# Modulation vectors summed along the free dimension on VectorE, with the result channels on partitions

## The chip, the cores and the metric

The kernel runs on one core of one Trainium2 chip. The metric is the device time of one launch, in microseconds (us). The core's engines are TensorE (PE, with its weight loads as a row of their own, PEld), VectorE (DVE), ScalarE (ACT), GpSimd (POOL) and SyncE (SP); here SP issues all loads. Each engine works through its own queue in order and waits where a semaphore tells it to.

## The reference

Four transformer layers (Fourier mixer, differential attention, latent attention, Fourier mixer, each followed by an MLP) over 256 latent and 256 context tokens of width 1024, then a second block with a mixture of experts. Each layer is steered by six modulation vectors per stream, and these are what the change is about:

```
sh_a, sc_a, g_a, sh_m, sc_m, g_m = split(silu(c)    @ mod_w[i] + mod_b[i], 6)   # latent stream
csh_a, ... , cg_m                = split(silu(c_ctx) @ mod_w[i] + mod_b[i], 6)   # context stream
h     = rms_norm(x, norm_mix_g[i]) * (1 + sc_a) + sh_a
x     = x + g_a * mixer(h)
x     = x + g_m * (relu(modulate(x, norm_mlp_g[i], sh_m, sc_m) @ w1)**2 @ w2)
```

`mod_w[i]` is 1024 x 6144 in fp32, 24 MB a layer. Layer 3 needs no context stream, and layer 2 needs only the first two vectors of it.

## The kernel before

Activations lie with channels on partitions: `x` is eight tiles of 128 channels x 512 tokens. Large products are made from split operands: every weight unit (128 x 1024) is loaded as `raw`, ACT casts it to `whi`, DVE subtracts to get `wlo`, and three matmuls (L377 to L379) make each product. An MLP (`mlp`) runs over eight chunks of 512 hidden channels. In a chunk `up` makes four groups `gk` of 24 matmuls of 512 columns; ACT takes relu and square, and ACT and DVE split the result into `hid` (L698). Then `down` makes eight groups `dn` of 12 matmuls of 512 columns, and after each of them DVE adds into `x` in two halves (L603). So a chunk has 192 matmuls on PE, and on DVE 16 `wlo` halves, four `hid` and 16 `x` additions. A `dn` group sits in one of three PSUM banks of tag "a". The order is `up(c+1)` ahead of `down(c)`.

The modulation vectors come in three ways:
- Layer 0, vectors 0 to 4, during the first Fourier mixer: `mod_steps` multiplies on PE (L524), with silu(c) as the stationary operand and weight tiles as the moving one.
- Layer 0, vector 5, by the same `mod_steps`, as a filler of the first MLP.
- Layers 1 to 3, by `mod_sums`, as a filler of the MLPs of layers 0 to 2. A tile of weights (128 input channels x 1024 results) is multiplied by silu(c), one number per partition, and added into `macc`: the first of eight tiles on ACT (L581), the others on DVE (L586), once per stream that needs it. What is left is a sum over the 128 partitions: matmuls with the 0/1 matrix `pick` (L592), an ACT copy out of PSUM (L595), four transposes (L545) and a DVE addition of the bias (L548).

A filler is a generator: `mlp` calls `next(fill)` after each `up` group and after each quarter of `down`, so many times as the layer's numbers say (one call at each place in layer 0, two at each `up` group of its first chunk). For layer 0 this makes 64 calls. Each `mod_sums` call works on one loaded tile of 512 KB; four such tiles (`mraw`) are in flight.

The queues' final order isn't the program's: a scheduler orders the instructions of each engine by a simulated timeline, and `issue_after` holds the fillers' DVE work behind the `hid` subtraction named by `s.anchors`. The order shown below is what came out of it.

Of the kernel before, what the change touches and what calls it, by code (L numbers as in the profile page):

```python
# [12 lines left out]
F32 = mybir.dt.float32  # L13
# [3 lines left out]
ALU = mybir.AluOpType  # L17
# [3 lines left out]
P = 128  # L21
# [11 lines left out]
MOD_STEP = 1024  # L33
# [171 lines left out]
def prepare(i, stages=ALL):  # L205
# [5 lines left out]
    a["mod_w"] = i["mod_w"]  # L211
# [101 lines left out]
class Builder:  # L313
    def __init__(s, ctx, tc, a, out, stages, dump):
# [28 lines left out]
        s.scale, s.behind = None, []  # L343
        s.csilu = s.fix.tile([P, 2 * NT + 30], F32, name="csilu")
        nc.vector.memset(s.csilu, 0.0)
        nc.scalar.activation(s.csilu[:, :2 * NT].rearrange("p (k r) -> p k r", r=2), s.cond, AF.Silu)
        s.pick = s.fix.tile([P, 33], F32, name="pick")
        nc.vector.memset(s.pick, 0.0)
        nc.vector.memset(s.pick[:, 1:2], 1.0)
        s.modt, s.amod = {}, {}  # L350
# [152 lines left out]
    def mod_steps(s, l, pool, parts=((0, 1), (2, 3), (4, 5)), bufs=4):  # L503
# [4 lines left out]
        def load():  # L508
            if order:
                c, kt = order.popleft()  # L510
                raws.append(pool.tile([P, UC], F32, name=f"mw{l}_{c}{kt}", tag="mraw", bufs=bufs))
                s.mod_dma = nc.sync.dma_start(raws[-1], s.a["mod_w"][l, kt * P:(kt + 1) * P, c * UC:(c + 1) * UC])
# [42 lines left out]
    def mod_sums(s, l, pool, cs=(0, 1, 2), bufs=4):  # L555
# [3 lines left out]
        raws, order = deque(), deque((c, kt, z) for c in cs for kt in range(NT) for z in range(2))  # L559

        def load():
            if order:
                c, kt, z = order.popleft()
                raws.append(pool.tile([P, UC], F32, name=f"mw{l}_{c}{kt}{z}", tag="mraw", bufs=bufs))
                c0 = c * 2048 + z * UC
                nc.sync.dma_start(raws[-1], s.a["mod_w"][l, kt * P:(kt + 1) * P, c0:c0 + UC])
# [4 lines left out]
        for c in cs:  # L571
            streams = range(2 if l == 1 or (l == 2 and c == 0) else 1)
            acc = [pool.tile([P, 2048], F32, name=f"macc{l}_{c}{r}", tag=f"macc{r}", bufs=1) for r in streams]
            for kt in range(NT):
                for z in range(2):
                    w = raws.popleft()
                    for r in streams:
                        a, k = acc[r][:, z * UC:(z + 1) * UC], s.csilu[:, 2 * kt + r:2 * kt + r + 1]
                        if kt == 0:
                            with s.tc.issue_after(s.anchors[0]):  # L580
                                nc.scalar.activation(a, w, AF.Copy, scale=k)  # L581
                        else:
                            for h in range(0, UC, MOD_STEP):
                                v = slice(h, h + MOD_STEP)
                                with s.tc.issue_after(s.anchors[1]):
                                    nc.vector.scalar_tensor_tensor(a[:, v], w[:, v], k, a[:, v], op0=ALU.mult, op1=ALU.add)  # L586
                    load()
                    yield
            ps = s.bank(f"mod{l}_{c}", "a")
            for r in streams:  # L590
                for j in range(4):
                    nc.tensor.matmul(ps[32 * j:32 * j + 32, :], s.pick[:, 1 - r:33 - r], acc[r][:, j * TOK:(j + 1) * TOK],  # L592
                                     start=r == 0, stop=r == len(streams) - 1, skip_group_check=True)
            sb = s.fix.tile([P, TOK], F32, name=f"modsb{l}_{c}", tag="tmp", bufs=4)
            nc.scalar.copy(sb, ps)  # L595
            yield
            s.mod_rows(l, 2 * c, 2, sb)
            yield
# [185 lines left out]
    def fourier(s, l, n, fill):  # L784
        nc, j = s.nc, l // 3
        modt = s.modt[l]
        with s.tc.tile_pool(name=f"four{l}", bufs=1) as ph:
# [58 lines left out]
            nc.vector.tensor_mul(gb, modt[:, 16:24, :], fb[:, j, :].unsqueeze(2).to_broadcast([P, NT, 2]))  # L846
# [1246 lines left out]
```

## Time and profile before

| | |
|---|---|
| median of 3 runs | 2010.93 us (2009.3 to 2012.24) |
| profiled execution: time, span | 2013.72 us, 2011.8 us |
| PE busy | 1962.1 us (98%) |
| PEld busy | 1671.6 us (83%) |
| DVE busy | 1481.2 us (74%) |
| ACT busy | 1100.8 us (55%) |
| mean granted TensorE clock | 0.99 |
| loads | 338.40 MB, 169 GB/s over the span |

The span runs from the first to the last instruction; 1.9 us of the execution lie around it. The chain of work that ended last goes 93% of the span through PE, mostly through `gk` and `dn` matmuls. The MLP of layer 0 begins at about 150 us and ends at about 510 us, that of layer 1 goes from about 770 to 1130 us, that of layer 2 from about 1290 to 1460 us. The profile puts an engine's busy time beside the length of a stretch, the idle time before an instruction in square brackets with what ended it, and merges neighbours of one kind into one row (x4).

### The profile page before, as it was taken

How to read it: one execution, taken by the hardware profiler on the slowest of the kernel's cores; microseconds unless marked ns; L12 is line 12 of the kernel's file. 1: busy time of each engine (PE TensorE's matmuls, PEld its weight loads, DVE VectorE, ACT ScalarE, POOL GpSimd, SP SyncE). 2: the span in 40 equal slices, each digit the busy share in tenths (PEclk: the TensorE clock that was granted, in tenths of full speed). 3: DMA queues.
4: the chain of work that ended last, by engine and by line, in shares of the span. 5: the costliest groups of instructions: out<-in, count | busy, mean ns of one | idle time of the engine just before them, and what ended most of it. 6: DMA issues, size and time to landing. Idle time of an engine off the chain costs nothing.

```text
span 2011.8 us, 31733 instructions
## 1 busy us (share of the span) xinstructions
PE 1962.1 (98%) x11858; PEld 1671.6 (83%) x11858; DVE 1481.2 (74%) x2832; ACT 1100.8 (55%) x2182; POOL 4.8 (0%) x13
## 2 busy tenths in 40 slices
PE   7999999999999999999999989999999999999997
PEld 4577878788888888877777977899999999987886
DVE  3645867687888956976666687788767777757698
ACT  4635333433678736343433377675657666565576
POOL 0000000000000000000000000000000000000000
PEclk9999999999999999999999999999999999999999
DMA  7845555453221223777665221576526655327694
GB/s 263 311 163 183 179 168 182 143 175 101 93 74 61 76 67 114 221 243 242 225 229 168 70 74 43 193 275 225 178 83 194 198 183 179 122 65 294 201 364 165
DMA packets 98108, 341.51 MB, mean 170 GB/s; under 512 B 13075, under 2 KB 14371, under 8 KB 97955
## 3 DMA queue, kind: packets, MB, share of 16 engines
q1 hardware_dynamic: 97954, 339.49, 50.7%
q8 instruction: 93, 1.52, 0.3%
q14 instruction: 61, 0.49, 0.1%
HBM read 338.40 MB, written 1.05 MB: 169 GB/s over the span
## 4 chain that ended last, share of the span: by engine, by line
PE 93%; DVE 3%; DMA 2%; ACT 1%; issue 1%; SPq 0%; DVEq 0%; ACTq 0%
PE gk L377 11%; PE gk L378 11%; PE gk L379 11%; PE dn L377 9%; PE dn L378 9%; PE dn L379 9%; PE gu L377 2%; PE gu L378 2%; PE gu L379 2%; PE mod L524 2%; PE pj L379 1%; PE pj L377 1%; PE pj L378 1%; DMA mw<-mod_w 1%; PE y L377 1%; PE y L378 1%
## 5 line engine op out<-in xcount | busy, mean ns | idle before, releaser
L369 ACT CAST whi<-raw 128x512 fp32r<-128x512 f32 (+1 forms) x731 | 430.8, 638 | 405.8 <-PE dn L379 276.1
L370 DVE TENSOR_TENSOR wlo<-raw,whi 128x512 fp32r<-128x512 f32 (+1 forms) x731 | 490.5, 708 | 107.4 <-ACT whi L369 105.1
L377 PE MATMUL gk<-hhi,whi 128*128 128x512 f32 (+2 forms) x1312 | 433.2, 333 | 3.1 <-ACT hhi L369 1.0
L378 PE MATMUL gk<-hhi,wlo 128*128 128x512 f32 (+2 forms) x1312 | 431.1, 330 | 0.2 <-DVE wlo L370 0.2
L379 PE MATMUL gk<-hlo,whi 128*128 128x512 f32 (+2 forms) x1312 | 425.4, 331 | 0.4 <-DVE hlo L468 0.4
L377 PE MATMUL dn<-hid,whi 128*128 128x256 f32 (+1 forms) x1088 | 356.7, 328 | 0.4 <-DVE x L603 0.4
L378 PE MATMUL dn<-hid,wlo 128*128 128x256 f32 (+1 forms) x1088 | 355.7, 327 | 0.0
L379 PE MATMUL dn<-hid,whi 128*128 128x256 f32 (+1 forms) x1088 | 355.1, 327 | 0.0
L377 PEld LDWEIGHTS gk<-hhi,whi 128*128 128x128 f32 x1312 | 247.8, 189 | 37.9 <-issue 4.6
L378 PEld LDWEIGHTS gk<-hhi,wlo 128*128 128x128 f32 x1312 | 248.5, 189 | 29.4 <-issue 5.0
L603 DVE SCALAR_TENSOR_TENSOR x<-dn,modt,x 128x256 f32<-128x256 f32 x384 | 174.0, 478 | 133.5 <-PE dn L379 133.3
L379 PEld LDWEIGHTS gk<-hlo,whi 128*128 128x128 f32 x1312 | 245.3, 189 | 30.8 <-issue 4.2
L586 DVE SCALAR_TENSOR_TENSOR macc<-mw,csilu,macc 128x1024 f32<-128x1024 f32 x182 | 226.4, 1276 | 1.7 <-DMA mw<-mod_w 1.7
L377 PEld LDWEIGHTS dn<-hid,whi 128*128 128x128 f32 x1088 | 204.4, 188 | 23.4 <-ACT whi L369 1.7
L378 PEld LDWEIGHTS dn<-hid,wlo 128*128 128x128 f32 x1088 | 204.8, 188 | 21.7 <-issue 1.7
L379 PEld LDWEIGHTS dn<-hid,whi 128*128 128x128 f32 x1088 | 204.0, 188 | 20.4
L695 ACT ACTIVATE relu<-gk 128x512 f32<-128x512 f32 x64 | 38.1, 595 | 108.8 <-PE gk L379 108.7
L698 DVE TENSOR_TENSOR hid<-relu,hid 128x512 fp32r<-128x512 f32 (+1 forms) x128 | 71.0, 554 | 31.4 <-ACT hid L698 29.6
L698 ACT CAST hid<-relu 128x512 fp32r<-128x512 f32 (+1 forms) x128 | 65.6, 513 | 41.9 <-PE dn L378 38.9
L697 ACT ACTIVATE relu<-relu 128x512 f32<-128x512 f32 (+1 forms) x128 | 67.2, 525 | 1.9
L392 ACT ACTIVATE sq<-x 128x256 f32<-128x256 f32 x104 | 41.5, 414 | 33.0 <-DVE x L603 25.9
L377 PE MATMUL pj<-hhi,whi 128*128 128x512 f32 (+1 forms) x144 | 54.0, 379 | 2.2 <-ACT hhi L467 2.2
(620 smaller groups left out, 3173.8 us busy)
## 6 DMA issues: line engine op xcount, KB each, us to landing
raw<-ws SPq DMA_DIRECT2D x378, 512.0 KB, 4.3
mw<-mod_w SPq DMA_DIRECT2D x192, 512.0 KB, 4.5
x<-ws SPq DMA_DIRECT2D x36, 512.0 KB, 5.4
more<-ws SPq DMA_DIRECT2D x24, 512.0 KB, 5.3
xt<-x SPq DMA_DIRECT2D x4, 512.0 KB, 4.8
raw<-ws SPq DMA_DIRECT2D x8, 256.0 KB, 2.5
out<-ht SPq DMA_DIRECT2D x4, 256.0 KB, 2.1
raw_dft_ch<-dft_ch SPq DMA_DIRECT2D x2, 384.0 KB, 4.1
```

Of the source, the lines that this page charges most:

```text
L369: s.nc.scalar.copy(hi, src)
L370: return s.nc.vector.tensor_sub(lo, src, hi.bitcast(F32))
L377: s.nc.tensor.matmul(out, lh, rh, start=f, stop=False)
L378: s.nc.tensor.matmul(out, ll, rh, start=False, stop=False)
L379: last = s.nc.tensor.matmul(out, lh, rl, start=False, stop=l)
L392: s.nc.scalar.activation(new, src, AF.Square)
L524: nc.tensor.matmul(ps[32 * j:32 * j + 32, :n], s.csilu[:, 2 * kt:2 * kt + 32], ws[j * m // 4][:, j * n % UC:j * n % UC + n], start=kt == 0 ...
L586: nc.vector.scalar_tensor_tensor(a[:, v], w[:, v], k, a[:, v], op0=ALU.mult, op1=ALU.add)
L603: s.nc.vector.scalar_tensor_tensor(s.x[:, ct, c], ps[:, c], gates[:, ct, q:q + 1], s.x[:, ct, c], op0=ALU.mult, op1=ALU.add)
L695: nc.scalar.activation(r[:, :n], ps[:, :n], AF.Relu)
L697: nc.scalar.activation(q[:, :n], r[:, :n], AF.Square)
L698: s.anchors = nc.scalar.copy(hid[c][0][:, m], q[:, :n]).ins, nc.vector.tensor_sub(hid[c][1][:, m], q[:, :n], hid[c][0][:, m].bitcast(F32)).ins
```

## The change

All of `mod_w` is handed over a second time, transposed, as `mod_wT` (result channels as rows). `mod_sums` now loads 128 result channels x 1024 input channels. `crow` holds silu(c) of each stream as a row of 1024 numbers, the same on all partitions; 16 small matmuls make it at the start, and ACT copies it out of PSUM in four pieces. One DVE instruction (L590 of the changed kernel) multiplies a tile with `crow` and adds along the free dimension; the sums land in their place in `modt`. `macc`, `pick`, the matmuls with it, the PSUM copy and the transposes are gone for layers 1 to 3, and so is ACT's part. Each of the six vectors is eight tiles; then the bias is added for the streams that were made. Vector 5 of layer 0 is made this way too. The last MLP that has a filler (layer 2) takes vectors 4 and 5 of layer 3, the one of layer 1 all of layer 2 and vectors 0 to 3 of layer 3. A mixer of layer 3 uses only the latent column of its gates. The count of loaded tiles stays at 192.

```diff
-    a["mod_w"] = i["mod_w"]
+    a["mod_w"] = i["mod_w"][stages[0] % 4]
+    a["mod_wT"] = i["mod_w"].transpose(0, 2, 1)
...
+    def cond_rows(s):
+        nc = s.nc
+        s.crow = s.fix.tile([P, 2, D], F32, name="crow")
+        for q in range(4):
+            ps = s.bank(f"crow{q}", "a")
+            for k in range(4):
+                c = 2 * (q % 2 * 4 + k) + q // 2
+                nc.tensor.matmul(ps[:, k * P:(k + 1) * P], s.csilu[:, c:c + 1].to_broadcast([P, P]), s.ident,
+                                 start=True, stop=True)
+            nc.scalar.copy(s.crow[:, q // 2, q % 2 * TOK:(q % 2 + 1) * TOK], ps)
...
+    def mod_sums(s, l, pool, vectors=range(6), bufs=4):
...
-        for c in cs:
-            streams = range(2 if l == 1 or (l == 2 and c == 0) else 1)
...
-                            with s.tc.issue_after(s.anchors[0]):
-                                nc.scalar.activation(a, w, AF.Copy, scale=k)
...
-                                    nc.vector.scalar_tensor_tensor(a[:, v], w[:, v], k, a[:, v], op0=ALU.mult, op1=ALU.add)
...
+        for c in vectors:
+            streams = range(2 if l < 2 or (l == 2 and c < 2) else 1)
+            n = len(streams)
+            for j in range(NT):
+                w = raws.popleft()
+                for r in streams:
+                    t = pool.tile([P, D], F32, name="msum", tag="msum", bufs=1)
+                    with s.tc.issue_after(s.anchors[1]):
+                        nc.vector.scalar_tensor_tensor(t, w, 1.0, s.crow[:, r], op0=ALU.mult, op1=ALU.mult,
+                                                       accum_out=s.modt[l][:, 8 * c + j, r:r + 1])
+                load()
+                if j < NT - 1:
                     yield
-            ps = s.bank(f"mod{l}_{c}", "a")
-            for r in streams:
-                for j in range(4):
-                    nc.tensor.matmul(ps[32 * j:32 * j + 32, :], s.pick[:, 1 - r:33 - r], acc[r][:, j * TOK:(j + 1) * TOK],
...
-            nc.scalar.copy(sb, ps)
-            yield
-            s.mod_rows(l, 2 * c, 2, sb)
+            m = s.modt[l][:, 8 * c:8 * c + 8, 0:n]
+            with s.tc.issue_after(s.anchors[1]):
+                nc.vector.tensor_add(m, m, s.mod_b[:, l, 8 * c:8 * c + 8].unsqueeze(2).to_broadcast([P, NT, n]))
...
-                    filler = lambda ph, f=filler: chain(s.mod_steps(0, ph, ((5,),)), f(ph))
+                    filler = lambda ph, f=filler: chain(s.mod_sums(0, ph, (5,)), f(ph))
...
-                    filler = lambda ph: chain(s.mod_sums(2, ph), s.mod_sums(3, ph, (0, 1)))
+                    filler = lambda ph: chain(s.mod_sums(2, ph), s.mod_sums(3, ph, range(4)))
...
-                    filler = lambda ph: s.mod_sums(3, ph, (2,))
+                    filler = lambda ph: s.mod_sums(3, ph, (4, 5))
```

Two places in DVE's queue and one in ACT's show what moves. First DVE before the first `x` addition of the first MLP, as it was:

```order
L698 TENSOR_TENSOR hid_1_1619<-relu_1647,hid_1_1618 128x512
L370 TENSOR_TENSOR wlo_1697<-raw_1544,whi_1696 128x512 x2
L548 TENSOR_TENSOR modt_117<-modtp_5_1692,c_mod_b 128x16
L698 TENSOR_TENSOR hid_1_1619<-relu_1688,hid_1_1618 128x512
L370 TENSOR_TENSOR wlo_1752<-raw_1569,whi_1751 128x512 x2
L698 TENSOR_TENSOR hid_1_1619<-relu_1731,hid_1_1618 128x512
L370 TENSOR_TENSOR wlo_1795<-raw_1616,whi_1794 128x512 x2
L603 SCALAR_TENSOR_TENSOR x<-dn_00_1802,modt_117,x 128x256 x2
```

The same place in the changed kernel (`msum` is the product tile that nobody reads, `modt_139` the vectors of layer 0):

```order
L702 TENSOR_TENSOR hid_1_1641<-relu_1769,hid_1_1640 128x512
L590 SCALAR_TENSOR_TENSOR msum,modt_139<-mw_55_1528,crow 128x1024 x2
L369 TENSOR_TENSOR wlo_1825<-raw_1638,whi_1824 128x512 x2
L590 SCALAR_TENSOR_TENSOR msum,modt_139<-mw_56_1551,crow 128x1024
L702 TENSOR_TENSOR hid_1_1641<-relu_1814,hid_1_1640 128x512
L590 SCALAR_TENSOR_TENSOR msum,modt_139<-mw_56_1551,crow 128x1024
L590 SCALAR_TENSOR_TENSOR msum,modt_139<-mw_57_1557,crow 128x1024
L369 TENSOR_TENSOR wlo_1863<-raw_1695,whi_1862 128x512 x2
L590 SCALAR_TENSOR_TENSOR msum,modt_139<-mw_57_1557,crow 128x1024
L597 TENSOR_TENSOR modt_139<-modt_139,c_mod_b 128x16
L590 SCALAR_TENSOR_TENSOR msum,modt_1673<-mw_00_1675,crow 128x1024
L607 SCALAR_TENSOR_TENSOR x<-dn_00_1832,modt_139,x 128x256 x2
```

From the first `hid` subtraction to the first `x` addition there are now 17 sums, 12 `wlo` halves and eight `hid` subtractions; before there were ten `wlo` halves, seven `hid` subtractions and no sum.

Next, DVE in the second `down` of that MLP, before:

```order
L603 SCALAR_TENSOR_TENSOR x<-dn_10_2186,modt_117,x 128x256 x2
L586 SCALAR_TENSOR_TENSOR macc_01_1746<-mw_060_2091,csilu,macc_01_1746 128x1024
L603 SCALAR_TENSOR_TENSOR x<-dn_11_2201,modt_117,x 128x256 x2
L586 SCALAR_TENSOR_TENSOR macc_00_1745<-mw_061_2134,csilu,macc_00_1745 128x1024
L370 TENSOR_TENSOR wlo_2217<-raw_2056,whi_2216 128x512 x2
L586 SCALAR_TENSOR_TENSOR macc_01_1746<-mw_061_2134,csilu,macc_01_1746 128x1024
L603 SCALAR_TENSOR_TENSOR x<-dn_20_2228,modt_117,x 128x256 x2
L370 TENSOR_TENSOR wlo_2259<-raw_2099,whi_2258 128x512 x2
L603 SCALAR_TENSOR_TENSOR x<-dn_21_2243,modt_117,x 128x256 x2
```

And now:

```order
L607 SCALAR_TENSOR_TENSOR x<-dn_10_2235,modt_139,x 128x256 x2
L590 SCALAR_TENSOR_TENSOR msum,modt_1673<-mw_11_1918,crow 128x1024
L607 SCALAR_TENSOR_TENSOR x<-dn_11_2250,modt_139,x 128x256 x2
L590 SCALAR_TENSOR_TENSOR msum,modt_1673<-mw_12_1962,crow 128x1024
L369 TENSOR_TENSOR wlo_2266<-raw_2099,whi_2265 128x512 x2
L590 SCALAR_TENSOR_TENSOR msum,modt_1673<-mw_12_1962,crow 128x1024
L607 SCALAR_TENSOR_TENSOR x<-dn_20_2279,modt_139,x 128x256 x2
L590 SCALAR_TENSOR_TENSOR msum,modt_1673<-mw_13_2006,crow 128x1024
L607 SCALAR_TENSOR_TENSOR x<-dn_21_2294,modt_139,x 128x256 x2
```

The pattern is the same; the sums are spread over all of the chunk, where before they stood closer together and paused at the first tiles and at the evacuations.

Last, ACT at the start of the program, where the rows `xt` of the input are squared and normalised, before:

```order
L880 ACTIVATE sq,ss<-xt 128x512
L880 ACTIVATE sq,rs_137<-xt 128x512
L880 ACTIVATE sq,ss<-xt 128x512
L880 ACTIVATE sq,rs_137<-xt 128x512
L444 ACTIVATE rsq<-ss,eps 128x2
L369 CAST hhi<-xn 128x512
L369 CAST dft_half_95<-raw_dft_half 128x516
```

And now:

```order
L884 ACTIVATE sq,ss<-xt 128x512
L884 ACTIVATE sq,rs_159<-xt 128x512
L564 COPY crow<-crow_83 128x512
L884 ACTIVATE sq,ss<-xt 128x512
L884 ACTIVATE sq,rs_159<-xt 128x512
L564 COPY crow<-crow_89 128x512
L443 ACTIVATE rsq<-ss,eps 128x2
L564 COPY crow<-crow_95 128x512
L368 CAST dft_half_117<-raw_dft_half 128x516
```

Two `crow` copies stand ahead of the first root, a third ahead of the first table's cast.

## Rows read from the trace of the kernel before

**Rows 1.** Window: length; PE, PEld, DVE, ACT, POOL busy; clock, DMA, GB/s.
```profile
176.00:300.00 124.00, 124.00 (x538) 97.79 (x538) 89.77 (x132) 49.51 (x82) 0.00 (x0) 1.00 0.56 174
```

**Rows 2.** Groups of instructions: busy us, mean ns | idle before them.
```profile
L586 DVE SCALAR_TENSOR_TENSOR macc<-mw,csilu,macc 128x1024 f32<-128x1024 f32 x182 | 226.4, 1276 | 1.7 <-DMA mw<-mod_w 1.7
...
L592 PE MATMUL mod<-macc,pick 128*32 128x512 f32 x104 | 19.3, 602 | 0.0
...
L545 PE MATMUL modtp<-ident,modsb 128*128 128x128 f32 x48 | 7.4, 273 | 0.3 <-ACT modsb L530 0.3
L595 ACT COPY modsb<-mod 128x512 f32<-128x512 f32 x9 | 5.2, 582 | 19.1 <-PE mod L592 19.1
```

**Rows 3.** Timeline of PE around one vector pair's pick matmuls: start, length, instruction.
```profile
268.39 0.39 PE L379 MATMUL gk<-hlo,whi 128*128 128x512 f32 x1
268.71 1.05 PE L592 MATMUL mod<-macc,pick 128*32 128x512 f32 x4
269.70 0.50 PE L377 MATMUL gk<-hhi,whi 128*128 128x512 f32 x1
...
273.52 0.40 PE L378 MATMUL gk<-hhi,wlo 128*128 128x512 f32 x1
273.85 1.91 PE L592 MATMUL mod<-macc,pick 128*32 128x512 f32 x12
275.69 0.50 PE L379 MATMUL gk<-hlo,whi 128*128 128x512 f32 x1
```

**Rows 4.** Timeline of PE at the transposes that follow.
```profile
280.92 0.60 PE L545 MATMUL modtp<-ident,modsb 128*128 128x128 f32 x4
281.27 0.48 PE L377 MATMUL dn<-hid,whi 128*128 128x512 f32 x1
```

**Rows 5.** Timeline of PE at the matmuls of vector 5 of layer 0.
```profile
143.49 0.39 PE L377 MATMUL gk<-hhi,whi 128*128 128x256 f32 x1 [0.49 <-ACT hhi L467]
...
153.78 1.93 PE L524 MATMUL mod<-mw,csilu 128*32 128x256 f32 x30
155.64 0.50 PE L377 MATMUL gk<-hhi,whi 128*128 128x512 f32 x1
```

**Rows 6.** Windows of the start, columns as in the first group.
```profile
0.00:20.00 20.00, 11.04 (x37) 4.81 (x38) 11.58 (x39) 14.51 (x35) 0.70 (x6) 1.00 0.83 283
...
50.00:85.00 35.00, 31.53 (x197) 21.65 (x198) 24.40 (x54) 22.93 (x58) 0.00 (x0) 1.00 0.84 310
```

**Rows 7.** Timeline of DVE at a product that is also summed along the free dimension.
```profile
1804.40 0.67 DVE L1490 SCALAR_TENSOR_TENSOR sqr<-ht 128x512 f32<-128x512 f32 x1
...
1805.00 0.08 DVE L1490 DVE_READ_ACCUMULATOR sqr<-ht 128x1 f32 x1
...
1805.18 0.16 DVE L1534 TENSOR_TENSOR ss<-ss 128x2 f32<-128x2 f32 x1
```

**Rows 8.** Timeline of DVE in the first MLP: first evacuation, then one chunk's start to the next's.
```profile
158.60 0.68 DVE L698 TENSOR_TENSOR hid<-relu,hid 128x512 fp32r<-128x512 f32 x1
...
187.70 0.88 DVE L603 SCALAR_TENSOR_TENSOR x<-dn,modt,x 128x256 f32<-128x256 f32 x2 [0.37 <-PE dn L379]
...
232.46 0.88 DVE L603 SCALAR_TENSOR_TENSOR x<-dn,modt,x 128x256 f32<-128x256 f32 x2 [0.37 <-PE dn L379]
233.25 0.68 DVE L698 TENSOR_TENSOR hid<-relu,hid 128x512 fp32r<-128x512 f32 x1
233.85 4.87 DVE L586 SCALAR_TENSOR_TENSOR macc<-mw,csilu,macc 128x1024 f32<-128x1024 f32 x4
238.63 0.87 DVE L603 SCALAR_TENSOR_TENSOR x<-dn,modt,x 128x256 f32<-128x256 f32 x2
239.42 1.27 DVE L586 SCALAR_TENSOR_TENSOR macc<-mw,csilu,macc 128x1024 f32<-128x1024 f32 x1
240.61 1.28 DVE L370 TENSOR_TENSOR wlo<-raw,whi 128x512 fp32r<-128x512 f32 x2
241.82 2.47 DVE L586 SCALAR_TENSOR_TENSOR macc<-mw,csilu,macc 128x1024 f32<-128x1024 f32 x2
```

More of the change, by code (lines that the diff above doesn't have):

```diff
@@ L32 @@
 META = 16
-MOD_STEP = 1024
 MORE = 3
@@ L343, in __init__ @@
         s.scale, s.behind = None, []
+        s.modt, s.amod = {}, {}
         s.csilu = s.fix.tile([P, 2 * NT + 30], F32, name="csilu")
@@ L346, in __init__ @@
         nc.scalar.activation(s.csilu[:, :2 * NT].rearrange("p (k r) -> p k r", r=2), s.cond, AF.Silu)
[L347 to L350, printed above, removed]
+        if stages[0] < 4:
+            s.cond_rows()
         s.acc = {}
@@ L511, in load @@
                 raws.append(pool.tile([P, UC], F32, name=f"mw{l}_{c}{kt}", tag="mraw", bufs=bufs))
-                s.mod_dma = nc.sync.dma_start(raws[-1], s.a["mod_w"][l, kt * P:(kt + 1) * P, c * UC:(c + 1) * UC])
+                s.mod_dma = nc.sync.dma_start(raws[-1], s.a["mod_w"][kt * P:(kt + 1) * P, c * UC:(c + 1) * UC])
         s.mod_tiles(l)
@@ L553, in mod_rows @@
                                                g[:, l, :].unsqueeze(2).to_broadcast([P, NT, 2]), op0=ALU.add, op1=ALU.mult)
-    def mod_sums(s, l, pool, cs=(0, 1, 2), bufs=4):
+    def cond_rows(s):
         nc = s.nc
-        raws, order = deque(), deque((c, kt, z) for c in cs for kt in range(NT) for z in range(2))
+        s.crow = s.fix.tile([P, 2, D], F32, name="crow")
[8 more added lines that the diff above has]
+        nc = s.nc
+        raws, order = deque(), deque((c, j) for c in vectors for j in range(NT))
         def load():
             if order:
[L563 to L566, printed above, removed]
+                c, j = order.popleft()
+                raws.append(pool.tile([P, D], F32, name=f"mw{l}_{c}{j}", tag="mraw", bufs=bufs))
+                r0 = c * D + j * P
+                nc.sync.dma_start(raws[-1], s.a["mod_wT"][l, r0:r0 + P])
         s.mod_tiles(l)
@@ new lines, in mod_sums @@
+        for c in vectors:
[10 more added lines that the diff above has]
+                if j < NT - 1:
+                    yield
+            m = s.modt[l][:, 8 * c:8 * c + 8, 0:n]
+            with s.tc.issue_after(s.anchors[1]):
+                nc.vector.tensor_add(m, m, s.mod_b[:, l, 8 * c:8 * c + 8].unsqueeze(2).to_broadcast([P, NT, n]))
+                if c in (1, 4):
+                    g = (s.g_mix, s.g_mlp)[c // 4]
+                    nc.vector.scalar_tensor_tensor(s.amod[l][:, c // 4, :, 0:n], m, 1.0, g[:, l, :].unsqueeze(2).to_broadcast(
+                        [P, NT, n]), op0=ALU.add, op1=ALU.mult)
@@ L845, in fourier @@
                 pass
-            nc.vector.tensor_mul(gb, modt[:, 16:24, :], fb[:, j, :].unsqueeze(2).to_broadcast([P, NT, 2]))
+            nc.vector.tensor_mul(gb[:, :, 0:1], modt[:, 16:24, 0:1], fb[:, j, :].unsqueeze(2))
             s.gemm_k8(n, s.biased(gb, modt[:, 16:24]), src=(fhi, flo), after=s.late_norm(l))
```

14 lines of the change are left out of this document (removed).

## The prediction

> **What bounds the kernel now.** I read the page's first part and the chain that ended last, then the windows, then the groups by line, and last the timelines of PE and DVE around the work that the change touches. In the first MLP PE is busy for all 124.00 us of a window, at full clock, while DVE is busy for 89.77 and ACT for 49.51 [rows 1]. One chunk there takes 44.76 us, from the first addition into x of one to that of the next (187.70 to 232.46), for 192 matmuls, so 0.233 us a matmul [rows 8]. PE is the bound of that stretch, and what is taken off its queue there shortens it, as long as DVE, which gets more to do, keeps up. ACT only loses work and isn't near its limit.
>
> **What leaves PE.** The pick matmuls stand between product matmuls without any idle time ahead of them. From the start of the product matmul before to the start of the one behind there are 1.31 us for four records and 2.17 us for twelve; less the 0.233 that the first matmul takes anyway that is 1.08 and 1.94, so 3.02 us for sixteen [rows 3]. There are 104 such records, which makes 19.6 us; their busy time, 19.3, says the same [rows 2]. The transposes hold up the next product by 0.35 us a group [rows 4], and nine groups go: 3.2 us. Of vector 5 of layer 0, thirty records in one row push the next product back by 1.86 us [rows 5]. Two records more and two transposes stand alone between products; I put them at 0.5, an estimate by the rows just used. The other 32 records of that vector lie where PE also waits for the normalised input (0.49 idle at 143.49, ended by ACT [rows 5]); at the rate of the thirty they would be worth 2.0, and I take 0.7, with 0 and 2.0 as ends. Sum: 19.6 + 3.2 + 1.9 + 0.5 + 0.7 = 25.9 us off PE's path. The evacuating ACT copies (582 ns, nine of them [rows 2]) go too, at no gain, since ACT isn't late there.
>
> **What comes at the start.** Sixteen small matmuls and four ACT copies for crow. PE is busy for only 11.04 of the first 20 us, ACT for 14.51 [rows 6], so the matmuls cost nothing and the copies may cost something: they are 512 columns wide like the copies of 582 ns [rows 2], together 2.3 us, and two stand ahead of the root that the first normalised rows wait for, a third ahead of the cast of the first table. Behind them on ACT wait the casts, and for these PE's first transform matmuls. Some of it comes back from 50 to 85 us, where PE is idle for 3.5 us and the DMA engines have their highest share, 0.84 [rows 6]: PE waits for weights there, and a delay before it shortens that wait. I take +1.0, with 0 and 2.3 as ends.
>
> **What DVE gets.** Sums were 182 and are now 16 + 96 + 64 + 48 = 224. The old one starts every 1.195 us (four from 233.85 to 238.63 [rows 8]). The new one is shown by the trace at half its width: a product of 512 columns that is also summed starts at 1804.40, the reading of its accumulator follows at 1805.00, and the next instruction, which needs the sum, starts at 1805.18, so 0.78 us in all [rows 7]. Another 512 columns cost at most half of 1.195, which gives 1.38 as the upper end; the lower is 1.195 and the 0.08 of the reading, 1.28. I take 1.32. The next sum waits for the one before, since both write the same tile msum, but that wait is in the 0.78.
>
> In a steady chunk DVE then has sixteen sums (21.1 us), eight pairs of x additions at 0.79 (238.63 to 239.42), eight pairs of wlo halves at 1.21 (240.61 to 241.82) and four hid subtractions at 0.60 (233.25 to 233.85) [rows 8]: 21.1 + 6.3 + 9.7 + 2.4 = 39.5 of 44.76 us. It fits, with 5 us to spare. That DVE may run without a pause and PE not notice is shown: from 232.46 to 241.82 DVE never waits, and four sums stand between two x additions, while the window shows PE fully busy [rows 1, 8]. The break-even is a sum of (44.76 - 18.4) / 16 = 1.65 us.
>
> [...] The product just shown has two fp32 sources in SBUF and is summed, and takes 0.60 us to its accumulator reading for 512 columns [rows 7], the old sum 1.195 for 1024 with two such sources [rows 8]; neither is at half rate, though the two sources of the first are one and the same tile. [...]
>
> One place is tight: the first up of the first MLP. Vector 5 must be ready before the first x addition, and DVE's order puts 17 sums, 12 wlo halves and 8 hid subtractions from the first hid subtraction to it: 17 x 1.32 + 12 x 0.605 + 8 x 0.60 = 34.5 us. Before, this stretch went from 158.60 to 187.70 [rows 8]. With the matmuls of vector 5 gone I let it begin at 156, so the first x addition starts at 190.5 and ends at 191.3. PE finishes the first dn about 3 us earlier than before, at 184.6, and can run two more (12 x 0.233 = 2.8 each) before it needs that bank again, at 190.2. PE stands for about 1 us, and DVE's waits for ACT in between add to it. I take +2.0, ends 0 and 5. What waits behind the sums on DVE there, besides x, is wlo of later weights; up to five units are split ahead, so this is not late first.
>
> In the second MLP the vectors with two streams come first, 32 sums in 16 calls, in 14 calls a chunk: 42.2 + 18.4 x 16/14 = 63.2 us in 51.2. Before there were 28 there and PE was as busy; the scheduler's order lets the new sums trail, and the later ones, one a call, leave room (14 x 1.32 + 18.4 = 36.9 of 44.76). I cost it at nothing; if its cover goes, up to 6 us are lost (12 behind, less two dn of slack). The loads are the same 192 tiles of 512 KB through the same four buffers, and the rows of 4 KB stay: nothing.
>
> **Sum.** -25.9 + 1.0 + 2.0 = -22.9 us. Against the profiled execution's own 2013.72 (span 2011.8 and 1.9 around it) that is 1990.8; that execution lies 2.8 above the median of the runs, 2010.93, so for the median 1988.0. The own range of this case is 1982 to 1996: the lower end has the crow copies and the stand for nothing and 2.0 for the uncertain records, and some gain from bank "a", which the pick matmuls no longer hold; the upper end has the copies at 2.3, the stand at 5 and some microseconds in the second MLP.
>
> **Rivals.** First, DVE takes most of it back. Its queue is in order, and an x addition that waits for PE makes the sums behind it late; 2.5 us lost in each of eight chunks of the first two MLPs would be 20, so 2008. For it: DVE is to go from 72% of the window to 88% of a chunk. Against it: the same pattern ran there before without a wait of PE. That the removed matmuls only filled waits of PE would end at the same place; the rows show no idle time around them [rows 3].
>
> Second, it gains more than the sum. ACT loses 26 multiplications and ten PSUM copies, and the dn groups get the third bank back whenever a pick group held it. If small waits that the busy times hide go with them, 8 to 10 us more, so 1979. Against it: PE was busy for all of the window, so few waits can be there.
>
> Third, slower: the sum runs at half rate. Two different fp32 tiles are read, and the trace shows the sum only with one tile read twice. A sum would then take 2 x 1.195 + 0.08 = 2.47 us, over the break-even of 1.65. A chunk of the first MLP would take 16 x 2.47 + 18.4 = 57.9 us instead of 44.76, over six chunks 79 us; its start 17 x 2.47 + 12.1 = 54.1 instead of 34.5, 20 us; the second MLP 96 x 2.47 + 7 x 18.4 = 366 instead of 313, 53 us. Less the 25.9 that is +126, so 2137 for the median.
>
> **Chances.** The forecast 0.74, more gain 0.07, taken back or hidden 0.12, half rate 0.07. Of the third group I count 0.05 as faster, 0.04 as within 0.2% (about what a measurement of this kernel tells from no change, 4 us) and 0.03 as slower. So faster 0.86, same 0.04, slower 0.10. The range for 8 in 10 is 1980 to 2005: it holds nearly all of the forecast, some of the gain beyond it and of what is taken back, and leaves out the half rate.
>
> **What would show it.** Right: PE's count of records lower by 104 + 64 + 38 and higher by some 32 at the start; the sums at about 1.2 us with a reading of 0.08 behind each, starting every 1.3 us; DVE near 88% of a steady chunk, PE without waits on DVE but at the first x addition of the first MLP; the second MLP shorter by about 11 us (48 of the 104 records at 3.02 for sixteen, and five of the nine groups of transposes). Wrong: sums of over 1.65 us, PE waits on x or wlo in several chunks, or a first mixer that ends some microseconds later than before.

## The result, and the profile after

The changed kernel takes 1985.45 us (median of 4 runs, 1982.98 to 1986.46), the kernel before on the same chip 2010.12 (4 runs). The ratio is 0.9866, 95% interval 0.9854 to 0.9879: 24.7 us faster, where 22.9 were forecast. The profiled execution took 1984.99 (span 1983.2). That of before (2013.72) lies 3.6 us above its median here and that of after 0.5 below its own, so the spans of the two traces differ by 28.6.

The page's first part, kernel after:

```profile
PE 1936.1 (98%) x11684; PEld 1670.4 (84%) x11684; DVE 1525.1 (77%) x3105; ACT 1070.5 (54%) x2150; POOL 4.8 (0%) x13
```

PE has 174 records fewer (11,858 before): the 104, 64 and 38 that were counted, less 32 for `crow`. The groups of DVE by line, kernel after (busy us, mean ns | idle before), answer to the old sums of [rows 2]:

```profile
L590 DVE SCALAR_TENSOR_TENSOR msum<-mw,crow 128x1024 f32<-128x1024 f32 x224 | 273.2, 1220 | 2.2 <-DMA mw<-mod_wT 1.0
...
L590 DVE DVE_READ_ACCUMULATOR msum<-mw,crow 128x1 f32 x224 | 18.7, 84 | 0.0
```

The old sum's mean was 1276 ns. Reading the accumulator is 84 ns of its own. DVE's timeline in the first MLP of after (start, length, instruction) shows what these cost in the queue, beside [rows 7, 8]:

```profile
197.01 1.22 DVE L590 SCALAR_TENSOR_TENSOR msum<-mw,crow 128x1024 f32<-128x1024 f32 x1
198.16 0.09 DVE L590 DVE_READ_ACCUMULATOR msum<-mw,crow 128x1 f32 x1
198.28 1.23 DVE L590 SCALAR_TENSOR_TENSOR msum<-mw,crow 128x1024 f32<-128x1024 f32 x1
...
202.39 1.22 DVE L590 SCALAR_TENSOR_TENSOR msum<-mw,crow 128x1024 f32<-128x1024 f32 x1
203.54 0.08 DVE L590 DVE_READ_ACCUMULATOR msum<-mw,crow 128x1 f32 x1
203.54 0.69 DVE L369 TENSOR_TENSOR wlo<-raw,whi 128x512 fp32r<-128x512 f32 x1
```

From a sum to the next sum, which writes the same tile, there are 1.27 us (197.01 to 198.28); to the start of its accumulator reading 1.15 (202.39 to 203.54). Another instruction, here a `wlo` subtraction, starts together with that reading, so beside other work a sum costs 1.15. The forecast was 1.32. Nothing is at half rate: a plain subtraction of two fp32 tiles of 1024 columns takes 1222 ns in this trace (36 of them, L369), as long as the sum.

The windows of after (length; PE, PEld, DVE, ACT, POOL busy; clock, DMA, GB/s): the stretch that answers to [rows 1], a later one, the first MLP from its first dn to its last, and the second MLP, from its normalisation (the first `st_mlp` matmul) to its last dn:

```profile
174.00:298.00 124.00, 124.00 (x533) 100.05 (x532) 116.34 (x216) 41.43 (x74) 0.00 (x0) 1.00 0.63 208
300.00:400.00 100.00, 100.00 (x430) 80.60 (x429) 86.12 (x158) 36.01 (x65) 0.00 (x0) 1.00 0.61 196
180.98:496.13 315.15, 315.15 (x1452) 258.69 (x1451) 262.21 (x492) 111.57 (x205) 0.00 (x0) 1.00 0.53 173
749.20:1115.80 366.60, 365.40 (x1756) 302.98 (x1755) 287.62 (x559) 140.33 (x264) 0.00 (x0) 1.00 0.61 201
```

The same two stretches of the MLPs in the kernel before:

```profile
184.70:509.96 325.26, 324.86 (x1512) 260.59 (x1511) 244.82 (x370) 123.71 (x218) 0.00 (x0) 1.00 0.51 160
763.50:1142.90 379.40, 378.21 (x1825) 305.20 (x1825) 275.82 (x446) 155.10 (x281) 0.00 (x0) 1.00 0.59 194
```

DVE is busy for 94% of the first stretch, and PE still for all of it: the list of PE's waits has no entry there. The first MLP is 10.1 us shorter from its first dn on (325.26 less 315.15) with DVE busy for 17 us more, the second 12.8 us (379.40 less 366.60) with DVE busy for 12 us more; its last dn in the kernel before is at 1142.9, later than the 1130 named above.

Where the 28.6 us lie shows by the same instruction in both traces, each the difference from one mark to the next: from the start to the first MLP's normalisation -2.1, on to its first dn -1.7, to the end of that MLP -10.1, second MLP -12.7, third -1.0. These are 27.6. The rest, -1.4 in the third mixer, -1.5 in the fourth and +3.1 in the fourth MLP among it, lies in code that the change leaves alone but for one DVE multiplication of gates in the fourth mixer. The steps in the mixers go with the granted clock: the fourth mixer takes 48.83 us at a mean clock of 0.93 in before, 47.32 at 0.96 in after and 45.79 at 1.00 in the last run below; the third 148.56 at 0.99 in before and 147.14 at 1.00 in after. The step in the fourth MLP doesn't, since the clock is at 1.00 there in every trace: from its normalisation to its last dn it takes 178.4 to 178.8 us in the four traces with the code of before, and 180.3 to 181.6 in all of those with the code of after but one (178.4, the run with the PE work put back). So it goes with the changed kernel; why is open. Single traces tell a stage with the change in it, but not the end to better than 3 us.

One thing was not foreseen. PE's timeline of after at the first MLP's normalisation, where vector 5 was before:

```profile
137.01 0.95 PE L418 MATMUL st_mlp<-ones,sq 128*128 128x2 f32 x8
139.26 1.19 PE L433 MATMUL r_mlp<-ident,rs_mlp 128*128 128x128 f32 x4 [1.30 <-DVE rs_mlp L451]
141.56 0.58 PE L376 MATMUL gk<-hhi,whi 128*128 128x256 f32 x1 [1.11 <-ACT hhi L466]
...
144.29 0.41 PE L377 MATMUL gk<-hhi,wlo 128*128 128x256 f32 x1
144.50 0.41 PE L376 MATMUL gk<-hhi,whi 128*128 128x256 f32 x1
...
146.26 0.28 PE L376 MATMUL gk<-hhi,whi 128*128 128x256 f32 x1
146.39 0.28 PE L377 MATMUL gk<-hhi,wlo 128*128 128x256 f32 x1
```

The windows of that stretch in after (columns as above):

```profile
138.00:140.00 2.00, 0.74 (x3) 0.77 (x4) 0.72 (x5) 0.26 (x1) 0.00 (x0) 0.81 0.96 385
140.00:142.00 2.00, 0.89 (x5) 0.59 (x4) 1.51 (x4) 1.00 (x3) 0.00 (x0) 0.50 0.90 365
142.00:144.00 2.00, 2.00 (x11) 2.00 (x11) 2.00 (x6) 1.06 (x3) 0.00 (x0) 0.50 0.03 12
144.00:146.00 2.00, 2.00 (x12) 2.00 (x11) 2.00 (x6) 1.17 (x3) 0.00 (x0) 0.50 0.00 0
146.00:148.00 2.00, 2.00 (x18) 2.00 (x18) 0.97 (x3) 0.51 (x1) 0.00 (x0) 0.99 0.00 0
```

The granted clock falls to 0.50 at about 139.2, at the end of the first wait (windows of 0.5 us have 1.00 until 139.0, 0.73 from there and 0.50 from 139.5), so the second wait isn't its reason. It is back at 146.0. Products of 256 columns start every 0.21 us meanwhile, and every 0.12 once it is back. From 141.56 to 146.00 that costs about 2 us, an estimate from these two spacings (4.44 us less 0.12/0.21 of it). In the kernel before, the same five windows have 1.00. It is no accident of one trace: all eight traces with the code of after show the lower clock between 132 and 148, and none of the four with the code of before.

### The profile page after: what moved, and what is told of

It is laid out like the page before. It is cut to its first block, busy times and chain, and to the rows that moved or that the text cites. A ratio compares the mean times of both kernels' runs of the same rounds, so it can differ in the third digit from the quotient of the medians.

```text
span 1983.2 us, 31614 instructions
## 1 busy us (share of the span) xinstructions
PE 1936.1 (98%) x11684; PEld 1670.4 (84%) x11684; DVE 1525.1 (77%) x3105; ACT 1070.5 (54%) x2150; POOL 4.8 (0%) x13
## 3 DMA queue, kind: packets, MB, share of 16 engines
HBM read 338.40 MB, written 1.05 MB: 171 GB/s over the span
## 4 chain that ended last, share of the span: by engine, by line
PE 94%; DVE 3%; ACT 2%; DMA 1%; issue 1%; SPq 0%; DVEq 0%; ACTq 0%
PE gk L376 11%; PE gk L377 11%; PE gk L378 11%; PE dn L377 9%; PE dn L376 9%; PE dn L378 9%; PE gu L376 2%; PE gu L377 2%; PE gu L378 2%; PE mod L523 2%; PE pj L376 1%; PE pj L378 1%; PE pj L377 1%; PE y L376 1%; PE y L377 1%; PE y L378 1%
## 5 line engine op out<-in xcount | busy, mean ns | idle before, releaser
L369 DVE TENSOR_TENSOR wlo<-raw,whi 128x512 fp32r<-128x512 f32 (+1 forms) x731 | 494.4, 711 | 111.0 <-ACT whi L368 109.1
L590 DVE SCALAR_TENSOR_TENSOR msum<-mw,crow 128x1024 f32<-128x1024 f32 x224 | 273.2, 1220 | 2.2 <-DMA mw<-mod_wT 1.0
L702 DVE TENSOR_TENSOR hid<-relu,hid 128x512 fp32r<-128x512 f32 (+1 forms) x128 | 71.0, 555 | 26.5 <-ACT hid L702 24.7
L391 ACT ACTIVATE sq<-x 128x256 f32<-128x256 f32 x104 | 41.6, 415 | 33.2 <-DVE x L607 25.9
```

Source lines behind the costliest of these rows:

```text
L369: return s.nc.vector.tensor_sub(lo, src, hi.bitcast(F32))
L391: s.nc.scalar.activation(new, src, AF.Square)
L590: nc.vector.scalar_tensor_tensor(t, w, 1.0, s.crow[:, r], op0=ALU.mult, op1=ALU.mult, accum_out=s.modt[l][:, 8 * c + j, r:r + 1])
L702: s.anchors = nc.scalar.copy(hid[c][0][:, m], q[:, :n]).ins, nc.vector.tensor_sub(hid[c][1][:, m], q[:, :n], hid[c][0][:, m].bitcast(F32)).ins
```

## The experiments

Theory: PE bounds both kernels in the MLPs, so the time that the removed records put between products comes off the end, and DVE's added work is hidden as long as a sum stays under 1.65 us. First rival: the records only filled slack, and the gain is ACT's or that of something freed. Second rival: DVE is already at the edge. Where a run is set against the kernel after (1985.45), the two medians come from different sessions; the kernel before moved by up to 2.3 us between these (2010.12 to 2012.41), so such a difference is no better than that.

**The pick groups and transposes twice** (kernel before). The last argument of `mod_rows` is new and says how often the transposes are issued.

```diff
-            for r in streams:
+            for r in (*streams, *streams):
                 for j in range(4):
                     nc.tensor.matmul(ps[32 * j:32 * j + 32, :], s.pick[:, 1 - r:33 - r], ...
...
-            s.mod_rows(l, 2 * c, 2, sb)
+            s.mod_rows(l, 2 * c, 2, sb, 2)
```

> The kernel before, with every pick group issued twice into the same bank and each group of transposes behind it twice; ACT and DVE do the same work as before, and the vectors come out the same. If the change gained by taking matmuls off PE's queue (my theory), the second issue costs what the first one does: 19.6 + 3.2 = 22.8 us more than before, about 2033, and PE shows the second group at about the same spacing. If the gain came mostly from ACT's lost work and from the PSUM bank and evacuation (rival), PE's extra groups cost less than 8 us.

Measured: 2028.4 us, before 2012.41, ratio 1.007 (1.0051 to 1.0088), so +16.0: between the two. PE's timeline in it, at the second half of the first pair's group:

```profile
276.46 0.40 PE L378 MATMUL gk<-hhi,wlo 128*128 128x512 f32 x1
276.79 3.63 PE L592 MATMUL mod<-macc,pick 128*32 128x512 f32 x28
280.35 0.50 PE L379 MATMUL gk<-hlo,whi 128*128 128x512 f32 x1
```

The 28 records put 3.89 us between the products (276.46 to 280.35), 3.66 over the 0.233 of one; the 12 of before put 1.94 [rows 3]. So 16 more records joined on cost 1.72, not 3.02. Summed over the trace, the spacing around picks grows by 11.2 us and that around transposes by 3.9: 15.1 against the measured 16. The three MLPs that hold them are 5.8, 7.4 and 1.4 us longer than before, 14.6 together. What stands in PE's queue does come out in the time; only the second issue was cheaper than I had said.

**The same work put back into the kernel after**, with no reader: the pick matmuls read `crow`, the transposes as well.

```diff
...
+            if l and c % 2:
+                ps = s.bank(f"mod{l}_{c}", "a")
+                for r in streams:
+                    for j in range(4):
+                        nc.tensor.matmul(ps[32 * j:32 * j + 32, :], s.pick[:, 1 - r:33 - r], s.crow[:, j % 2, ...],
+                                         start=r == 0, stop=r == n - 1, skip_group_check=True)
+                tp = s.bank(f"modtp{l}_{c}", "b")
+                for q in range(4):
+                    nc.tensor.transpose(tp[:, q * P:(q + 1) * P], s.crow[:, 0, q * P:(q + 1) * P], s.ident)
```

> The changed kernel, with the 104 pick records and 36 transposes put back on PE after every second vector of layers 1 to 3, on data that lies in SBUF and with nobody reading the result; ACT and DVE as in the changed kernel. My theory: 22.8 us come back, about 2008, that is within 4 us of the kernel before. Rival (ACT and evacuations make the gain): under 8 us come back, 1993 or less.

Measured: 1995.07, ratio 0.9907 (0.989 to 0.9923), +9.6 over the kernel after: again too little for the theory as I had priced it, too much for the rival. PE's timeline in it:

```profile
253.53 0.40 PE L381 MATMUL dn<-hid,whi 128*128 128x512 f32 x1
253.86 1.93 PE L602 MATMUL mod<-crow,pick 128*32 128x512 f32 x16
255.71 0.50 PE L379 MATMUL gk<-hhi,whi 128*128 128x512 f32 x1
```

Here `crow` is ready at any time, so all 16 records stand in one place and cost 1.95 (2.18 less 0.233); in the kernel before they stood in two, 4 and 12, for 3.02 [rows 3]. Eight in one place cost 1.08. Four such groups of sixteen and five of eight make 13.2 us, and the first twelve transposes fell into PE's wait at 143. By the trace the first MLP is 5.2 us longer from its first dn to its last, the second 7.7 and the third 1.2. The PSUM bank is held here for the matmuls alone, since no ACT copy follows; what its longer hold in the kernel before cost is not tested by itself.

**The same in the kernel before, joined**: the quarters issued in an order in which the first two can't go ahead of the others.

```diff
-                for j in range(4):
+                for j in (2, 3, 0, 1):
                     nc.tensor.matmul(ps[32 * j:32 * j + 32, :], s.pick[:, 1 - r:33 - r], ...
```

> The kernel before, with the four quarters of a pick group issued in the order 2, 3, 0, 1, so that the first two can't be issued ahead of the other two, whose sums come later. In the kernel before six of nine groups stand in two places of PE's queue; here the three with one stream stand in one, those with two streams in one or two with eight records each. Theory (what a group costs PE is a price per place in its queue, about 1.08 for up to eight records and 1.95 for sixteen, so the shortfall of the run that put the picks back on PE comes from the joined groups): 3 x 1.07 + 3 x 0.86 = 5.8 us less, so about 2006, and the spacing of the products around the picks in its trace adds up to some 14 instead of 19.6. Rival (the price is one per record and the shortfall came from elsewhere, a gap of PE that hid them): the time of the kernel before, within 1 us, and a spacing of 19 to 20.

Measured: 2009.52, before 2011.69, ratio 0.9988 (0.9973 to 1.0003): the time does not decide; 2006 would be 0.9972, just outside. PE's timeline in it:

```profile
275.30 0.39 PE L379 MATMUL gk<-hlo,whi 128*128 128x512 f32 x1
275.62 1.06 PE L592 MATMUL mod<-macc,pick 128*32 128x512 f32 x8
276.61 0.50 PE L377 MATMUL gk<-hhi,whi 128*128 128x512 f32 x1
277.04 1.07 PE L592 MATMUL mod<-macc,pick 128*32 128x512 f32 x8
278.04 0.50 PE L378 MATMUL gk<-hhi,wlo 128*128 128x512 f32 x1
```

Sixteen records as twice eight cost 1.08 and 1.20, not 3.02. All picks together put 14.8 us between the products, where the kernel before has 19.6: the price of a place is shown in the spacing. The MLPs that hold most of them are 1.7 and 2.8 us shorter, 4.5 of the 4.8 that the spacing lost, and 2.0 of that is lost in the first mixer, which the edit doesn't touch: its granted clock is 0.50 for 6.9 us there (from 53.6), which it never is there in the trace of before.

**ACT's work put back** (kernel after): 26 multiplications of 1024 columns and nine copies of 512.

```diff
+                if l and j == 0:
+                    for r in streams:
+                        idle = pool.tile([P, D], F32, name="idle", tag="idle", bufs=1)
+                        with s.tc.issue_after(s.anchors[0]):
+                            nc.scalar.activation(idle, w, AF.Copy, scale=s.csilu[:, r:r + 1])
+                if l and c % 2 and j == 7:
...
+                        nc.scalar.copy(idle[:, :TOK], s.crow[:, 0, :TOK])
```

> The changed kernel, with ACT's part put back: 26 multiplications of 128 x 1024 and nine copies of 512 columns, in about the same places, with nobody reading the result (28.2 + 5.2 us of ACT busy time). My theory: ACT isn't near its limit, so no change, 1983 to 1988. Rival: 10 us or more come back, 1995 or more.

Measured: 1982.01, ratio 0.9851 (0.9834 to 0.9867). The 26 cost ACT 1150 ns each, 30 us in all, and the time doesn't rise: what ACT lost is worth nothing that can be seen. As far as it rests on ACT, the first rival falls.

**DVE's margin**: an instruction more on DVE behind each of the 224 sums, first of 128 columns.

```diff
                                                        accum_out=s.modt[l][:, 8 * c + j, r:r + 1])
+                        nc.vector.tensor_mul(t[:, :128], w[:, :128], s.crow[:, r, :128])
```

> The changed kernel, with one more DVE multiplication of 128 columns behind every sum (224 in all), into the same product tile. That makes a sum cost about 1.27 + 0.25 = 1.5 us on DVE, under the break-even of 1.65 that the prediction worked out for a steady chunk. My theory: DVE has about 5 us to spare in a chunk of 44.76, so only the start of the first MLP pays, 17 x 0.25 = 4 us at most: 1985 to 1990. Rival (DVE is already at its limit and the queue's order makes every addition show): 224 x 0.25 = 56 us on DVE, half or more of it in the time, 2013 or more.

Measured: 1989.97, ratio 0.9886 (0.9864 to 0.9908): 4.5 over the kernel after, with intervals that overlap. In its trace both MLPs are as long as in after within 0.3 us; what is later lies in the first mixer (1.3) and the third (5.3). The last sum of the second MLP ends 57 us ahead of the third mixer, so no sum stands in it; but its mean clock is 0.97 (152.40 us) where after has 1.00 (147.14): it is at 0.50 for 10 us in all, which loses some 5. Whether the added work brought that about is not shown.

And of 512 columns:

> The changed kernel, with one more DVE multiplication of 512 columns behind every sum. A sum then costs about 1.27 + 0.70 = 1.97 us, over the break-even of 1.65. My theory: a chunk of the first MLP takes 16 x 1.97 + 18.4 = 49.9 instead of 44.76, six of them 31 us; the start of it 17 x 0.7 = 12; the second MLP 96 x 1.97 + 7 x 18.4 = 318 instead of 313, 5; together 40 to 50 us more than the changed kernel, about 2030. Rival (DVE's spare time is larger than the sum says, since a reading of the accumulator lies beside the next instruction): under 25 us more, 2010 or less.

Measured: 2020.03, ratio 1.0044 (1.0029 to 1.0058), 34.6 over the kernel after. DVE's timeline in it, first MLP:

```profile
302.69 0.68 DVE L703 TENSOR_TENSOR hid<-relu,hid 128x512 fp32r<-128x512 f32 x1
303.29 0.68 DVE L592 TENSOR_TENSOR msum<-mw,crow 128x512 f32<-128x512 f32 x1
304.01 1.23 DVE L590 SCALAR_TENSOR_TENSOR msum<-mw,crow 128x1024 f32<-128x1024 f32 x1
```

The added instruction takes the queue for 0.72 us (303.29 to 304.01), so a sum costs about 1.87, over the break-even of 1.65; with 128 columns it was some 1.4 (0.20 to 0.32 for the added one). The loss is not where I looked for it. In the chunks PE goes on without a wait, since the sums trail: the first MLP is 314.5 us long from its first dn to its last (315.2 in after), the second 366.2 (366.6). The bill comes behind the MLP. Windows in this kernel from the last dn on:

```profile
496.00:505.00 9.00, 3.43 (x17) 3.27 (x18) 9.00 (x22) 3.04 (x8) 0.00 (x0) 0.77 0.58 176
505.00:515.00 10.00, 7.66 (x49) 7.00 (x48) 10.00 (x29) 2.71 (x6) 0.00 (x0) 0.87 0.17 54
```

And in the kernel after:

```profile
496.00:505.00 9.00, 6.59 (x49) 5.80 (x48) 8.38 (x26) 5.98 (x13) 2.08 (x4) 1.00 0.50 160
```

DVE is busy throughout while PE waits (by the list of waits 4.2 us for the next normalisation, and from 550 to 561 another 10.4 for `v`, which DVE splits). From the last dn of the first MLP to the second MLP's normalisation PE is idle for 24.7 us, where after has 5.6, and busy for 8.7 us more, at a mean clock of 0.96 for 0.99: part of the bill is that lower clock, 0.77 in the first of its windows above, with PE busy for 3.43 of 9 us. At the second MLP's normalisation the kernel is 27 us behind, at the end of that MLP still 27, and at the third's normalisation 37.

**Two tiles for the products instead of one** (kernel after), so that a sum needn't wait for the one before.

```diff
-                    t = pool.tile([P, D], F32, name="msum", tag="msum", bufs=1)
+                    t = pool.tile([P, D], F32, name="msum", tag="msum", bufs=2)
```

> The changed kernel with two product tiles instead of one. In its trace a sum that follows a sum starts 1.26 to 1.27 us after it, one that follows another instruction lets that one start after 1.15: if the difference is the wait for the one product tile, sums that follow each other now start every 1.15 us. In the time this is worth nothing by my theory (DVE isn't the bound), 1983 to 1988; if DVE bounds the first MLP's start, up to 2 us less.

Measured: 1983.88, ratio 0.9861 (0.9842 to 0.9881), no change. DVE's timeline in it:

```profile
199.34 1.23 DVE L590 SCALAR_TENSOR_TENSOR msum<-mw,crow 128x1024 f32<-128x1024 f32 x1
200.49 0.09 DVE L590 DVE_READ_ACCUMULATOR msum<-mw,crow 128x1 f32 x1
200.49 1.23 DVE L590 SCALAR_TENSOR_TENSOR msum<-mw,crow 128x1024 f32<-128x1024 f32 x1
```

The next sum starts together with the reading, after 1.15 us. The shared tile costs 0.12 a sum, on an engine that has room.

**`crow` alone** (kernel before, with `cond_rows` added, called at the start, and nothing reading what it makes).

```diff
         s.modt, s.amod = {}, {}
+        s.cond_rows()
...
```

> The kernel before, with the sixteen small matmuls and four ACT copies for crow added at the start and nobody using crow. The prediction's step: +1.0 us (0 to 2.3). The changed kernel's trace rather shows the first MLP's statistics 2.1 us earlier than before: if that is due to the new order of the first matmuls and not to crow, this kernel is between 2 us faster and 1 us slower than before, and its trace shows where the first transform product and the statistics of the first MLP stand (11.09 and 120.48 us before, 11.39 and 118.41 in the changed kernel).

Measured: 2011.42, before 2012.41, ratio 0.9997 (0.9986 to 1.0009). In the trace the first MLP's normalisation starts at 118.56 against 120.48 before, 1.9 earlier rather than later. PE's waits up to 55 us, kernel before (us in total, times, longest):

```profile
PE mod L524 <- DMA mw<-mod_w: 3.1, 3, 1.6
```

The same in this run:

```profile
PE mod L525 <- DMA mw<-mod_w: 1.1, 2, 0.6
```

PE waits 2.0 us less for weights of the first vectors, which agrees in size. But that mark isn't steady: over the kernels whose code is nearly the same up to it, it lies between 120.5 and 123.5 with the code of before, and between 118.4 and 121.4 with that of after (in part of them the granted clock falls to 0.50 on the way, for 6.9 us in the two late ones of before, 122.5 and 123.5). So `crow` costs nothing that can be seen; that it brings 2 us is not shown.

**Vector 5 back on PE** (kernel after).

```diff
-                    filler = lambda ph, f=filler: chain(s.mod_sums(0, ph, (5,)), f(ph))
+                    filler = lambda ph, f=filler: chain(s.mod_steps(0, ph, ((5,),)), f(ph))
```

> The changed kernel, with vector 5 of layer 0 made by matmuls as before. The prediction counts 3.1 us for taking it off PE (1.9 + 0.5 + 0.7), and 2.0 of them given back since PE waits for DVE at the first x addition: by that this kernel is 1 us slower than the changed one, and the first MLP's DVE has 16 sums less. The changed kernel's trace shows another loss: with these matmuls gone PE idles from 137.96 to 141.56, but for one small product, and its granted clock is 0.50 from 140 to 146, where it was 1.00 before. If that costs more than the matmuls do, this kernel is as fast or up to 2 us faster, and its trace shows the clock at 1.00 there.

Measured: 1988.32, ratio 0.9882 (0.9863 to 0.9902): 2.9 slower, within the intervals. That is nearer to the 1 us slower than to the rival, which also asked for a clock of 1.00 in its trace. From the normalisation to the first dn its trace is 2.8 longer than that of after, so taking the vector off PE is worth about that, the lower clock of either trace counted in. Windows in it:

```profile
142.00:144.00 2.00, 1.70 (x10) 1.35 (x6) 2.00 (x6) 1.34 (x4) 0.00 (x0) 0.50 0.97 346
144.00:146.00 2.00, 2.00 (x16) 1.10 (x16) 2.00 (x6) 1.34 (x3) 0.00 (x0) 0.73 0.86 348
```

The clock falls here too, for a shorter time. So that vector 5's records are gone is not the whole reason for the fall; why the kernel before kept 1.00 stays open. With the same records as before but this clock the stretch is 1.2 us longer than in before (65.4 for 64.2).

**One vector more** (kernel after): vector 4 of layer 0 by sums as well, in the first mixer, with its tiles in an area that is free there.

```diff
-            fill = s.mod_steps(0, ph, ((0, 1), (2,), (3, 4)))
+            area = []
+            fill = s.mod_first(ph, area)
...
+        for _ in s.mod_steps(0, ph, ((0, 1), (2,))):
+            yield
+        a, b = s.mod_steps(0, ph, ((3,),)), s.mod_sums(0, ph, (4,), 3, area)
+        for _ in a:
+            next(b, None)
+            yield
...
```

> The kernel after, and in the first Fourier mixer vector 4 of layer 0 is also computed by sums on DVE (16 more sums, tiles in an area of SBUF that is free there); vector 3 stays on PE, alone. PE then issues 8 groups of eight 256-column records instead of 16 groups of four 512-column records. Theory (PE is the bound of this stretch, it was busy for all of 60 to 118.4 us in the kernel after, and DVE has room, 28.6 of 58.4 us busy): 16 x about 1.05 less 8 x about 0.65, so some 11 us less on PE, of which 8 to 11 show in the time: 1974 to 1978. DVE's 16 sums are 16 x 1.2 = 19 us and fit. Rival: the sums lie ahead of DVE's part of the normalisation in its queue and make the MLP's input late; then the first MLP starts no earlier and the time is 1984 or more.

Measured: 1976.41, ratio 0.9824 (0.9805 to 0.9844), clear of the interval of the kernel after: the fastest kernel of this study. A window in it:

```profile
90.00:100.00 10.00, 10.00 (x65) 7.67 (x64) 8.62 (x21) 5.77 (x13) 0.00 (x0) 1.00 0.61 219
```

The same in the kernel after:

```profile
90.00:100.00 10.00, 10.00 (x40) 4.74 (x40) 3.38 (x8) 2.67 (x6) 0.00 (x0) 1.00 0.96 358
```

PE is full in both, but gets more products done where the vector's records are gone, and DVE has taken it into its free time. The first MLP begins 8.0 us earlier and its first dn 10.3, and this stays to the end of the third MLP.

## Why the prediction was right, point by point

**PE's removed work sets the gain: shown.** Doubled, put back and joined, it moved the time or the MLPs by about what the spacing in the trace said, and ACT's work moved nothing. The term of 19.6 for the picks was right as a sum, since the spacings of the kernel before do add up to that. The rate it came from, 3.02 for sixteen, was not: the price went by places, and in one place four or eight records cost 1.08 (eight that stood one product behind another group 1.20, in the joined run), twelve or sixteen 1.95, and 28, in the run that issues them twice, 3.66. Split groups of sixteen cost 3.02, one that stood in one place 1.95, the split single-stream ones 2.15 for eight. That these came out alike on the whole is chance. By it I expected 22.8 of the first two runs and got 16.0 and 9.6. Putting work back returned 9.6 us of the gain, and vector 5 another 2.9; that the rest of the picks' part is the price of split places rests on the spacings and the lengths of the MLPs, not on a time of the whole kernel.

**The second MLP shorter by 11: 12.7.** With the rates just given its five groups had 3.02 + 2.15 + 2.15 + 1.10 + 2.15 = 10.6, and five groups of transposes 1.8: 12.4. The first MLP had 3.02 + 3.02 + 1.95 and 1.05: 9.0, measured 10.1. What is left for anything else, the bank's longer hold included, is 1.1 us in the first and 0.3 in the second.

**The sum at 1.32: 1.15 to 1.27.** The accumulator's reading hides beside the next instruction, which [rows 7] could not show, since that next one needs the sum. DVE's busy share, named at 88% of a steady chunk, is 94% in the first stretch and 86% from 300 to 400. The break-even of 1.65 was not tested closely: at about 1.4 the MLPs lost nothing and the time 4.5 us, at 1.87 the time lost 34.6 us, but the MLPs again nothing, though by the sum each chunk should have grown. The sum is a balance of DVE's work; where sums may trail, it doesn't say where the loss will show. The third rival's half rate, 2.47 us a sum, was an assumption of mine that no run shows: with two different fp32 tiles a sum takes 1220 ns for 1024 columns, as long as a plain subtraction of two such tiles (1222 ns).

**The stand at the first `x` addition, +2.0: it fell away.** The addition starts at 191.40, later than the 190.5 forecast, but PE doesn't wait, because its order had changed too. PE's timeline of after:

```profile
189.38 0.39 PE L376 MATMUL gk<-hhi,whi 128*128 128x512 f32 x1
...
191.23 0.39 PE L378 MATMUL gk<-hlo,whi 128*128 128x512 f32 x1
191.47 0.40 PE L376 MATMUL gk<-hhi,whi 128*128 128x512 f32 x1
```

I had DVE's order and took PE's from the kernel before. The next up's gk stand there now, where I had put the dn that needs the bank.

**Vector 5, -3.1: -1.7 in that stretch by the trace.** Taking the records off was worth 2.8 against the run with them back, which has a lower clock of its own; the low clock takes about 2 of the stretch and was not in the sum. At full clock the records would be worth 3.7, an estimate from these two (1.7 + 2.0).

**The start, +1.0: wrong in sign, by the trace.** It is 2.1 earlier; how much of that is scatter stays open.

So the forecast of 22.9 met 24.7 with two terms of the other side that fell away (+2.0 and +1.0) and two losses that were not in it, about 2 us by the clock and 3.1 in the fourth MLP. In the stretches that lose PE work the traces show 25.5 (1.7 + 10.1 + 12.7 + 1.0), where the prediction had 25.9 less the 2.0 of the stand: the mechanism was right, that the whole came so close is in part luck. No rival took place; that of more gain would have been 1979, 6 us off.

## What to carry to other kernels

Where PE is full, price what leaves it by the spacing between its neighbours, place by place: here a group split over two places cost more than the same records in one, and a rate from one kind of group didn't hold for another. Before calling a step between two traces scatter, look at the granted clock of that stretch. An engine that gets the work is tested by adding to it until the time gives, and what it can't do in time may show up behind the loop, in the next normalisation and the mixer, not in the loop. Where the order is made by a scheduler, read the new order of the waiting engine as well as that of the working one.

## What the runs showed of the hardware

A product of 1024 fp32 columns with its sum along the free dimension takes DVE 1.22 us, and reading the sum 0.08, beside the next instruction unless that one writes the same tile (1.15 or 1.27 from start to start). Matmuls onto 32 rows of a bank: eight records on the four quarters cost 1.08 us in the joined run, what four on two quarters cost in the kernel before. In the kernel after PE's clock fell to 0.50 at the end of a wait of 1.30 us, ahead of which PE had done eight products of two columns, and stayed there for 6.8 us (139.2 to 146.0), the last 4.4 of them with PE busy throughout; products of 256 columns then started every 0.21 us where they start every 0.12. The fourth mixer, the same on PE in all kernels here, took 45.8, 47.3 and 48.8 us at a mean clock of 1.00, 0.96 and 0.93.
